# A hybrid decoder step on one core: 16-row instead of 32-row substitution on GpSimd, the keys' norm on ScalarE, and another order of steps

## The chip, the cores and the metric

One core of one Trainium2 chip. The metric is the device time of one execution in microseconds. Engines are called as in the profile: PE (TensorE, matmuls), DVE (VectorE), ACT (ScalarE), POOL (GpSimd), SP (SyncE, which here only issues transfers).

## What is computed

One inference step of a two-layer trunk, for a prompt of 512 tokens and a batch of 8 samples of 4 tokens (544 columns in all, model width 1024). Layer 0 mixes tokens by a gated delta rule (16 value heads, 8 key heads, 128 wide), layer 1 by sliding-window attention; after each comes a SwiGLU block. The delta rule, cut to what the change touches, is computed in chunks:

```
q, k = l2norm(q) * 128**-0.5, l2norm(k)
kb   = k * beta
Bm   = where(strict_lower, (kb @ k.T) * decay, 0)        # one matrix per chunk and head
T    = inverse of (I + Bm)                               # unit lower triangular
u    = T @ (v * beta);   w = T @ (kb * exp(G))
aqk  = (q @ k.T) * decay                                 # lower triangular
# then chunk by chunk, in order:
unew = u - w @ S
o    = (q * exp(G)) @ S + aqk @ unew
S    = S * exp(Gl) + (k * exp(Gl - G)).T @ unew
```

The kernel takes chunks of 128 tokens, so that 4 chunks x 16 heads = 64 matrices T of 128x128 are needed, 16 for each of four groups of 4 heads.

## The kernel before

All large products go through `dense` (L141): weights come by SP from memory in pieces of 128x512 (256 KB, `load_w` L129, three buffers `wr_*`), ACT casts each piece to a high part (`wh_*`, L134), DVE subtracts for the low part (`wl_*`, L136), and PE multiplies at L160 three times (hi x hi, lo x hi, hi x lo) over two halves of 256 and 288 columns. In names, `win` are the projections to q, k, v, `wz` those to the gate z, `wo` the output projection.

Layer 0 is done for four groups g = 0..3 of four heads. The string `PLAN` (L38) names the steps in the order in which the program writes them: `kq` projects queries and keys, `t` (`tphase`, L599) makes the matrices, `p` (`states`) feeds small products with the samples' states between the dense matmuls, `v` projects values, `s` is the sample's part, `m` (`merge`, L776) joins inverted blocks to whole T, `c` (`chain`, L840) goes through the four chunks, `z` projects the gates, `o` (`out`, L1024) normalizes and multiplies them. A tile framework then orders each engine's instructions by its own estimates; waits are semaphores, and an engine never passes an instruction that waits.

What `tphase` does for a group, in turn: PE transposes keys and queries (`pkt`), ACT squares them (`ssk`), 1/norm of the keys comes as `rk` from POOL (`rsqrt_col`, a power, L215), and its logarithm `lk` from ACT. From these DVE makes `cbk`, `ckd`, `R`, `Rh`, `RR`; PE transposes `RR` (`prr`, L663), then makes Gram matrices (`gram`, L685) and decays (`pe`, L689/691); ACT takes exponentials `E` (L697) and DVE writes `BA` (L698, both the matrix to invert and the causal one). SP copies the 32x32 diagonal blocks of `BA` to memory (`D1`, L703) and back with one block on each of 64 partitions, twice (`Lb`, L722). POOL inverts them by forward substitution in `Tn`, even columns on 64 partitions and odd ones on the other 64 (L726 to L735, the loop quoted below). DVE makes a transposed copy (L737, into `Lb`'s memory), SP writes both to memory (`D2`, L742/743) and reads them back in the places that merging needs: three transfers to `Tn` (L748; the tile's second half holds zeros, L745) and eight to `BA` (L752).

```
for j in range(31):
    r_, w = 31 - j, j // 2 + 1
    POOL.tensor_tensor(tv, Lb[:, j, j+1:32] ..., Tn[:, j, 0:w] ..., ALU.mult)
    POOL.tensor_tensor(Tn[:, j+1:32, 0:w], Tn[:, j+1:32, 0:w], tv, ALU.subtract)
```

`merge` works on two halves of a group, eight matrices each: 16 small matmuls `pw` (L791/792) multiply the block below the diagonal with the inverse above it, ACT negates to `W1` (L794), 24 matmuls `py` (L798 to 800) multiply with the other inverse, ACT copies to `BA` and `Tn`; then the same once more from 64 to 128 rows (`pw2` L812, `W2` L814, `py2` L818, `BA` L819). `chain` needs `BA` from its first matmul on (`pu`, L878; then `pS` L883, `po` L849, `pk` L864, `pq` L871).

`out` takes 1/norm of the outputs from POOL as well (`ro`, L1041, the same function at L215), ACT scales `Os` (L1042) and the outputs (L1051, names `KQ`) by it, and POOL issues transfers of results (`out_sp` L892, `out_ss` L1003, `ogsc` L1088).

Of the kernel before, what the change touches and what calls it, by code (L numbers as in the profile page):

```python
# [398 lines left out]
def gdn(ctx, tc, env):  # L399
# [199 lines left out]
    def tphase(q):  # L599
# [127 lines left out]
        for k in range(2):
            POOL.memset(TU[64 * k:64 * k + 64, 16 * k:512:33], 1.0)
        for j in range(31):
            r_, w = 31 - j, j // 2 + 1  # L730
            tt = p2.tile([P, 136], F32, tag="subt", name=f"subt{g}_{j}", bufs=1)
            tv = tt[:, :r_ * w].rearrange("p (a b) -> p a b", b=w)
            POOL.tensor_tensor(tv, Lb[:, j, j + 1:32].unsqueeze(2).to_broadcast([P, r_, w]),  # L733
                              Tn[:, j, 0:w].unsqueeze(1).to_broadcast([P, r_, w]), ALU.mult)
            POOL.tensor_tensor(Tn[:, j + 1:32, 0:w], Tn[:, j + 1:32, 0:w], tv, ALU.subtract)  # L735
# [814 lines left out]
```

## Time and profile before

| what | value |
|---|---|
| timed runs | 1718.17, 1713.74, 1734.78 us; median 1718.17 us |
| the profiled execution | 1713.87 us |
| its span | 1712.1 us |
| mean clock granted to PE in it | 0.971 |
| layer 0's delta part | 0 to about 700 us of the span |

The profile is of one execution. All times of rows are in us from the start of its span, unless ns is written. Nothing behind the first 700 us is touched by the change. The 1.8 us between span and execution time lie around the program.

### The profile page before, as it was taken

To read this page: it belongs to the slowest core of one execution; us is meant where nothing else is said; L and a number is where in the kernel's file an instruction comes from. 1 tells how busy PE (TensorE), PEld (TensorE's weight loads), DVE (VectorE), ACT (ScalarE), POOL (GpSimd) and SP (SyncE) were. 2 spreads that over 40 slices of the span, in tenths; PEclk is the share of its full clock that TensorE was granted. 3 is DMA by queue.
4 is the path that set the end of the run, shared out by engine and by line. 5 is a ranking of instruction groups with operands and counts; after the bars stand their busy time and mean duration, and the time that the engine had idled before them with its cause. 6 is when DMAs were issued, how large, how long until landed. Compare 5 with 4: busy or idle time off the path is not lost.

```text
span 1712.1 us, 34075 instructions
## 1 busy us (share of the span) xinstructions
PE 1614.7 (94%) x13370; PEld 1557.7 (91%) x13370; DVE 946.8 (55%) x2073; ACT 753.8 (44%) x1822; POOL 254.3 (15%) x484
## 2 busy tenths in 40 slices
PE   7997998899698798999999999999989999999997
PEld 6997897799588798999999999999779999999997
DVE  7986486477367456544444433457656444444233
ACT  5865485584565445433333323236544333333221
POOL 2318128117305200100000000000000000000001
PEclk9999899899799999999999999999999999999998
DMA  6224533533455564622222333453112222223322
GB/s 216 81 79 129 134 97 89 154 115 108 110 162 160 155 218 132 196 90 87 92 87 87 89 90 85 119 150 99 57 41 83 88 88 92 87 87 90 90 85 86
DMA packets 155506, 187.73 MB, mean 110 GB/s; under 512 B 59232, under 2 KB 83856, under 8 KB 155344
## 3 DMA queue, kind: packets, MB, share of 16 engines
q1 hardware_dynamic: 146960, 164.34, 32.6%
q0 software_dynamic: 4256, 14.67, 2.5%
q10 hardware_dynamic: 4128, 6.53, 1.3%
q8 instruction: 105, 1.72, 0.4%
q14 instruction: 57, 0.47, 0.1%
HBM read 155.23 MB, written 25.02 MB: 105 GB/s over the span
## 4 chain that ended last, share of the span: by engine, by line
PE 75%; POOL 8%; DMA 5%; DVE 4%; ACT 3%; issue 3%; SPq 1%; ACTq 0%; DVEq 0%; POOLq 0%
PE wu_p L160 15%; PE wg_p L160 15%; PE wd_p L160 14%; PE win_p L160 5%; PE wz_p L160 4%; PE wqkv_p L160 4%; POOL Tn L735 3%; POOL subt L733 3%; PE wao_p L160 3%; PE wo_p L160 2%; DMA xsc<-xr 1%; PE ptp L1279 1%; DMA Lb<-D 1%; PE gram L685 1%; PE po L1285 1%
## 5 line engine op out<-in xcount | busy, mean ns | idle before, releaser
L160 PE MATMUL wg_p<-hl,wh_wg 128*128 128x256 f32 (+1 forms) x704 | 199.8, 288 | 1.5 <-DVE hl L207 1.5
L160 PE MATMUL wu_p<-hl,wh_wu 128*128 128x256 f32 (+1 forms) x704 | 199.7, 288 | 0.0
L160 PE MATMUL wg_p<-hh,wl_wg 128*128 128x256 f32 (+1 forms) x704 | 199.1, 287 | 0.0
L160 PE MATMUL wu_p<-hh,wl_wu 128*128 128x256 f32 (+1 forms) x704 | 199.1, 287 | 0.0
L160 PE MATMUL wg_p<-hh,wh_wg 128*128 128x256 f32 (+1 forms) x704 | 198.5, 288 | 0.3 <-DVE g L330 0.3
L160 PE MATMUL wu_p<-hh,wh_wu 128*128 128x256 f32 (+1 forms) x704 | 198.8, 288 | 0.0
L160 PE MATMUL wd_p<-al,wh_wd 128*128 128x256 f32 (+1 forms) x660 | 190.4, 289 | 0.0
L160 PE MATMUL wd_p<-ah,wl_wd 128*128 128x256 f32 (+1 forms) x660 | 190.1, 288 | 0.0
L160 PE MATMUL wd_p<-ah,wh_wd 128*128 128x256 f32 (+1 forms) x660 | 188.1, 285 | 0.0
L136 DVE TENSOR_TENSOR wl_wd<-wr_wd,wh_wd 128x512 fp32r<-128x512 f32 x90 | 58.3, 648 | 151.8 <-ACT wh_wd L134 150.7
L160 PEld LDWEIGHTS wg_p<-hl,wh_wg 128*128 128x128 f32 x704 | 132.4, 188 | 1.7 <-DVE hl L207 1.7
L134 ACT CAST wh_wg<-wr_wg 128x512 fp32r<-128x512 f32 x88 | 54.7, 621 | 178.6 <-PE wu_p L160 128.0
L160 PEld LDWEIGHTS wg_p<-hh,wh_wg 128*128 128x128 f32 x704 | 132.3, 188 | 0.4 <-DVE g L330 0.4
L160 PEld LDWEIGHTS wg_p<-hh,wl_wg 128*128 128x128 f32 x704 | 132.6, 189 | 0.0
L160 PEld LDWEIGHTS wu_p<-hh,wl_wu 128*128 128x128 f32 x704 | 132.6, 189 | 0.0
L160 PEld LDWEIGHTS wu_p<-hh,wh_wu 128*128 128x128 f32 x704 | 132.4, 188 | 0.0
L160 PEld LDWEIGHTS wu_p<-hl,wh_wu 128*128 128x128 f32 x704 | 132.4, 188 | 0.0
L160 PE MATMUL win_p<-hl0n,wh_win 128*128 128x256 f32 (+1 forms) x448 | 131.7, 296 | 0.6 <-DVE hl0n L279 0.6
L160 PE MATMUL win_p<-hh0n,wl_win 128*128 128x256 f32 (+1 forms) x448 | 131.8, 297 | 0.0
L160 PE MATMUL win_p<-hh0n,wh_win 128*128 128x256 f32 (+1 forms) x448 | 131.2, 295 | 0.5 <-ACT pre L542 0.5
L134 ACT CAST wh_wd<-wr_wd 128x512 fp32r<-128x512 f32 x90 | 52.7, 585 | 174.9 <-PE wd_p L160 154.0
L160 PEld LDWEIGHTS wd_p<-al,wh_wd 128*128 128x128 f32 x660 | 124.1, 188 | 0.0
(453 smaller groups left out, 4489.6 us busy)
## 6 DMA issues: line engine op xcount, KB each, us to landing
wr_wg<-in_w_gu SPq DMA_DIRECT2D x88, 256.0 KB
wr_wu<-in_w_gu SPq DMA_DIRECT2D x88, 256.0 KB
wr_wd<-in_w_dn SPq DMA_DIRECT2D x75, 256.0 KB
wr_win<-in_w_in SPq DMA_DIRECT2D x64, 256.0 KB
Sgp<-in_sdelta SPq DMA_DIRECT2D x16, 512.0 KB
wr_wz<-in_w_in SPq DMA_DIRECT2D x32, 256.0 KB
Sgs<-in_sdelta SPq DMA_DIRECT2D x16, 512.0 KB
out_ss<-Sgs POOLq DMA_DIRECT2D x16, 512.0 KB, 4.2
```

Source lines behind the costliest of these rows:

```text
L134: ACT.copy(hi[:, :n], raw[:, o:o + n])
L136: DVE.tensor_tensor(lo[:, :n], raw[:, o:o + n], hi[:, :n], ALU.subtract)
L160: PE.matmul(ps[f][:m, :hw(f)], lhsT=wt[:, sl], rhs=xt[:, hc(f)], start=(k0 + j == 0 and wi == 0), stop=(k0 + j == total - 1 and wi == 2),)
L685: PE.matmul(gr[:, j * 256:(j + 1) * 256], lhsT=KQ[j][:, n, 0, :], rhs=KQ[j][:, n].rearrange("p a b -> p (a b)"), start=True, stop=True)
L733: POOL.tensor_tensor(tv, Lb[:, j, j + 1:32].unsqueeze(2).to_broadcast([P, r_, w]), Tn[:, j, 0:w].unsqueeze(1).to_broadcast([P, r_, w]), AL ...
L735: POOL.tensor_tensor(Tn[:, j + 1:32, 0:w], Tn[:, j + 1:32, 0:w], tv, ALU.subtract)
L1279: PE.transpose(ptp[:, c * 256 + kb * P:c * 256 + (kb + 1) * P], s[:, c, n, kb * P:(kb + 1) * P], ident)
L1285: PE.matmul(po[rows, n * P:(n + 1) * P], lhsT=vt[:, n - 1 + kb, kv * 64:kv * 64 + 64], rhs=pT[:, c, kb * P:(kb + 1) * P], start=(kb == k0 ...
```

## The change

Four edits, all in layer 0's delta part.

1. Substitution on 16 rows. The tile `LT` holds one 16x16 diagonal block on each of 128 partitions (first half the block, second half its inverse). The loop has 15 steps of two POOL instructions instead of 31. The memory tile `D2` (one for the plain and one for the transposed inverses) is now made once, with zeros between the 16-row blocks, which POOL writes at the program's start; SP reads the inverses back as 32x32 block-diagonal pieces, four transfers to `TU` and one to a new tile `DT` (transposed), and no longer to `BA`.
2. Joining 16 to 32 rows at the start of `merge`: 64 matmuls `pa`, one DVE instruction to `V` (which masks and negates), 112 matmuls `pz`, three DVE additions to `DT` and `TU`, eight POOL copies from `DT` to `BA` for the group. The rest of `merge` reads `DT` where it read the diagonal blocks of `BA`.
3. The keys' 1/norm `rk` is exp(-0.5 * lk) on ACT instead of a power on POOL.
4. Another `PLAN`. Smaller buffers pay for the new tiles (`VBB` 7 instead of 8, one buffer for `R`, `Rh`, `RR`, another tag for two small tiles).

```diff
-PLAN = ("ba kq0 rn gt t0 p0 v0 s0 m0 kq1 v1 c0 t1 p1 z0 kq2 o0 s1 m1 v2 p2 "
-        "c1 t2 z1 o1 kq3 s2 m2 v3 t3 c2 z2 p3 z3 o2 s3 m3 c3 wa wb o3")
+PLAN = ("ba kq0 rn gt t0 p0 kq1 v0 s0 m0 t1 p1 c0 v1 kq2 z0 o0 s1 m1 t2 "
+        "p2 c1 v2 kq3 z1 o1 s2 m2 t3 c2 v3 p3 z2 z3 o2 s3 m3 c3 wa wb o3")
...
+    D2 = [dpool.tile([16, 4, 2, 16, 32], F32, name=f"D2{t}", bufs=1) for t in "nt"]
...
+    zero = big("sub", "zero", 3)
+    POOL.memset(zero[:, :512], 0.0)
+    for t in range(2):
+        nc.gpsimd.dma_start(D2[t].rearrange("u b k s c -> (u b k) (s c)"), zero[:, :512])
...
         rk = p2.tile([P, 9], F32, tag="rk", name=f"rk{g}")
-        rsqrt_col(rk, ssk, 9)
         lk = p2.tile([P, 9], F32, tag="lk", name=f"lk{g}")
         ACT.activation(lk, ssk, AF.Ln)
+        ACT.activation(rk, lk, AF.Exp, scale=-0.5)
...
-        Lb = big("sub", f"Lb{g}", 3)
+        LT = q.LT = p2.tile([P, 2, 16, 16], F32, tag="LT", name=f"LT{g}", bufs=1)
+        Lb, Tn = LT[:, 0], LT[:, 1]
         for k in range(2):
-            nc.sync.dma_start(Lb[64 * k:64 * k + 64], D1.rearrange("b n h s c -> (b n h) (s c)"))
...
+            o = slice(16 * k, 16 * k + 16)
+            nc.sync.dma_start(Lb[64 * k:64 * k + 64], D1.rearrange("u b s c -> (u b) s c")[:, o, o])
         POOL.memset(Tn, 0.0)
+        POOL.memset(Tn.rearrange("p s c -> p (s c)")[:, 0:256:17], 1.0)
+        TU = q.TU = big("sub", f"TU{g}", 3).rearrange("p (u c) -> p u c", c=64)
+        POOL.memset(TU[0:64], 0.0)
+        for j in range(15):
+            r_, w = 15 - j, j + 1
+            tt = p2.tile([P, 64], F32, tag="subt", name=f"subt{g}_{j}", bufs=1)
+            tv = tt[:, :r_ * w].rearrange("p (a b) -> p a b", b=w)
+            POOL.tensor_tensor(tv, Lb[:, j, j + 1:16].unsqueeze(2).to_broadcast([P, r_, w]),
+                              Tn[:, j, 0:w].unsqueeze(1).to_broadcast([P, r_, w]), ALU.mult)
+            POOL.tensor_tensor(Tn[:, j + 1:16, 0:w], Tn[:, j + 1:16, 0:w], tv, ALU.subtract)
+        Tt = Lb
+        DVE.tensor_copy(Tt, Tn.rearrange("p a b -> p b a"))
...
+            for t, src in enumerate((Tn, Tt)):
+                nc.sync.dma_start(D2[t].rearrange("u b k s c -> k (u b) s c")[k][:, :, o], src[64 * k:64 * k + 64])
+        q.DT = p2.tile([P, 16, 32], F32, tag="DT", name=f"DT{g}", bufs=1)
+        nc.sync.dma_start(q.DT, D2[1].rearrange("u b k s c -> (b k s) u c"))
+        for b in range(4):
             o = 32 if b == 1 else 0
...
+            nc.sync.dma_start(TU[32 * b:32 * b + 32, :, o:o + 32], D2[0][:, b].rearrange("u k s c -> (k s) u c"))
...
-        g, TU = q.g, q.TU
+        g, TU, DT = q.g, q.TU, q.DT
+        blocks = [(u_, slice(32 * b, 32 * b + 32)) for u_ in range(16) for b in range(4)]
+
+        pa = bank("v", f"pa{g}")
+        for u_, bs in blocks:
+            o = 32 if bs.start == 32 else 0
+            PE.matmul(pa[bs, u_ * 32:u_ * 32 + 32], lhsT=q.BA[u_ // 8][bs, u_ // 4 % 2, u_ % 4, 0, bs],
+                      rhs=TU[bs, u_, o:o + 32], start=True, stop=True)
+        V = q.LT.rearrange("p a b c -> p (a b c)").rearrange("p (u c) -> p u c", c=32)
+        POOL.memset(V[:, :, 16:32], 0.0)
+        DVE.tensor_scalar(V[:, :, 0:16], pa.rearrange("p (u c) -> p u c", c=32)[:, :, 0:16], kc("partu"), -1.0,
+                          ALU.mult, ALU.mult)
+        pz = bank("v", f"pz{g}")
+        for u_, bs in blocks:
+            PE.matmul(pz[bs, 256 + u_ * 16:272 + u_ * 16], lhsT=V[bs, u_], rhs=DT[bs, u_, 16:32], start=True, stop=True)
+            if bs.start < 96:
+                PE.matmul(pz[bs, u_ * 16:u_ * 16 + 16], lhsT=DT[bs, u_], rhs=V[bs, u_, 0:16], start=True, stop=True)
+        pzv = pz.rearrange("p (t u c) -> p t u c", t=2, c=16)
+        DVE.tensor_tensor(DT[:, :, 16:32], pzv[:, 1], DT[:, :, 16:32], ALU.add)
+        DVE.tensor_tensor(TU[0:96, :, 0:16], pzv[0:96, 0], TU[0:96, :, 0:16], ALU.add)
+        DVE.tensor_tensor(TU[32:64, :, 32:48], pzv[32:64, 0], TU[32:64, :, 32:48], ALU.add)
+        for hf in range(2):
+            for b in (2, 3, 0, 1):
+                bs = slice(32 * b, 32 * b + 32)
+                POOL.tensor_copy(q.BA[hf][bs, :, :, 0, bs].rearrange("p n h c -> p (n h) c"), DT[bs, 8 * hf:8 * hf + 8])
```

Where the instructions now stand. PE before, in the middle of group 1's `tphase`: its first matmul `prr1` stands between dense matmuls of the gate projection z0 (the number behind a name's group is a head's, the last one a buffer's).

```order
L160 MATMUL wz0_2_p1_3154<-hh0n_4_632,wl_wz0_2_0_4_3165 128x288
L663 MATMUL prr1_2699<-kon_70,RR1_2694 68x128
L685 MATMUL gram1_0_2711<-KQ1_1791 128x256 x2
L160 MATMUL wz0_2_p1_3154<-hh0n_5_636,wh_wz0_2_0_4_3163 128x288
L160 MATMUL wz0_2_p1_3154<-hl0n_5_637,wh_wz0_2_0_4_3163 128x288
```

PE of the changed program at the same place (`pa0` is the first matmul of group 0's `merge`, the bulk of it stands here).

```order
L161 MATMUL win4_p0_3321<-hh0n_7_650,wh_win4_0_4_3331 128x256
L161 MATMUL win4_p0_3321<-hl0n_7_651,wh_win4_0_4_3331 128x256
L161 MATMUL win4_p0_3321<-hh0n_7_650,wl_win4_0_4_3333 128x256
L782 MATMUL pa0_1922<-TU0_931,BA0_0_824 32x32 x31
L782 MATMUL pa0_1922<-TU0_931,BA0_1_871 32x32 x32
L670 MATMUL prr1_2336<-kon_70,RR1_2331 68x128
L692 MATMUL gram1_0_2348<-KQ1_1023 128x256 x2
```

Group 0's joining has moved ahead of group 1's `tphase`: 187 dense matmuls (91 of 256 and 96 of 288 columns), 18 transposes and 8 small products stand between the last `pe0` and the first `pa0`; before, 127 `win`, 192 `wz`, 96 state products, `prr1` and a `gram1` stood between the last `pe0` and the first `pw0`.

POOL before, in group 1's substitution: `ro0`, the 1/norm of group 0's outputs, stands between the halves of a step.

```order
L733 TENSOR_TENSOR subt1_21_2882<-Lb1_2812,Tn1_2815 128x110
L735 TENSOR_TENSOR Tn1_2815<-Tn1_2815,subt1_21_2882 128x10x11
L733 TENSOR_TENSOR subt1_22_2885<-Lb1_2812,Tn1_2815 128x108
L215 TENSOR_TENSOR ro0_3704<-sso0_3666,mhalf_73 128x17
L735 TENSOR_TENSOR Tn1_2815<-Tn1_2815,subt1_22_2885 128x9x12
```

POOL of the changed program, from the last step of group 1's substitution to `ro0`.

```order
L741 TENSOR_TENSOR LT1_2449<-LT1_2449,subt1_14_2498 128x15
L556 COPY cso2_3158<-pre4_3383 128x3
L557 COPY cso2_3158<-pre4_3383 128x24
L785 MEMSET LT1_2449 128x16x16
L547 MEMSET pre5_3462 128x3
L548 COPY pre5_3462<-scst2_3159 128x8x3
L556 COPY cso2_3158<-pre5_3462 128x3
L557 COPY cso2_3158<-pre5_3462 128x24
L909 DMA out_sp<-S0_2543 128x4x128
L216 TENSOR_TENSOR ro0_3789<-sso0_3751,mhalf_73 128x17
```

`ro0` now comes after the whole substitution; the memset of `V` (L785) waits until SP's copies of the inverses have been read.

SP before, from group 1's blocks to the copies of its inverses: the weights of z1 are loaded ahead of the copies.

```order
L722 DMA Lb1_2812<-D1_1_2709 64x1024 x2
L129 DMA wr_win27_0_0_4280<-in_w_in 128x512
L129 DMA wr_win27_0_4_4282<-in_w_in 128x512
L129 DMA wr_wz1_0_0_0_4866<-in_w_in 128x512
L129 DMA wr_wz1_0_0_4_4868<-in_w_in 128x512
L129 DMA wr_wz1_1_0_0_4962<-in_w_in 128x512
L129 DMA wr_wz1_1_0_4_4964<-in_w_in 128x512
L900 DMA Sgp1_2_2957<-in_sdelta 128x4x256
L129 DMA wr_wz1_2_0_0_5058<-in_w_in 128x512
L900 DMA Sgp1_3_2959<-in_sdelta 128x4x256
L129 DMA wr_wz1_2_0_4_5060<-in_w_in 128x512
```

SP of the changed program at the same place.

```order
L730 DMA LT1_2449<-D1_1_2346 64x16x16 x2
L748 DMA D2n_192<-LT1_2449 64x16x16 x2
L748 DMA D2t_193<-LT1_2449 64x16x16 x2
L753 DMA TU1_2454<-D2n_192 32x16x32 x3
L750 DMA DT1_2506<-D2t_193 128x16x32
L753 DMA TU1_2454<-D2n_192 32x16x32
L130 DMA wr_wz0_1_0_0_3549<-in_w_in 128x512
L130 DMA wr_wz0_1_0_4_3551<-in_w_in 128x512
```

Nothing stands between `LT1` and the copies of its inverse, so the weights of z0's second head are issued only when the whole substitution and its way back are done. In group 2 the weights of z1's third head, in group 3 those of z3's third head stand behind the copies in the same way.

## Rows read from the trace of the kernel before

**Rows 1.** The page: busy time by engine, and the chain that ended last.
```profile
PE 1614.7 (94%) x13370; PEld 1557.7 (91%) x13370; DVE 946.8 (55%) x2073; ACT 753.8 (44%) x1822; POOL 254.3 (15%) x484
...
PE 75%; POOL 8%; DMA 5%; DVE 4%; ACT 3%; issue 3%; SPq 1%; ACTq 0%; DVEq 0%; POOLq 0%
```

**Rows 2.** Stretches: length, busy of PE, PEld, DVE, ACT, POOL; PE clock, DMA share, GB/s.
```profile
0.00:700.00 700.00, 623.63 (x5407) 582.45 (x5407) 455.16 (x1026) 406.30 (x1152) 233.23 (x445) 0.95 0.46 136
150.00:600.00 450.00, 394.05 (x3549) 365.46 (x3548) 271.93 (x621) 253.11 (x750) 174.61 (x339) 0.92 0.45 127
200.00:250.00 50.00, 48.89 (x381) 42.24 (x380) 37.39 (x92) 36.20 (x106) 7.67 (x21) 0.83 0.42 126
```

**Rows 3.** Waits of PE, 0 to 700 us: total, times, longest.
```profile
PE wz_p L160 <- ACT wh_wz L134: 16.3, 2, 9.1
PE pw L791 <- DMA Tn<-D: 13.9, 4, 6.6
PE prr L663 <- DVE RR L661: 8.7, 1, 8.7
...
PE wo_p L160 <- ACT wh_wo L134: 4.2, 1, 4.2
...
PE pw L792 <- DMA Tn<-D: 1.9, 2, 1.2
```

**Rows 4.** Waits of all engines, 0 to 700 us.
```profile
ACT Os L1042 <- POOL ro L215: 29.3, 3, 12.1
```

**Rows 5.** The chain that ended last, pieces between 126 and 296 us (start, duration).
```profile
127.03 0.41 DVE BA L698
...
135.80 0.67 POOL subt L733
...
163.97 1.79 POOL rk L215
...
177.36 3.69 DMA D<-Tn
...
181.15 4.15 DMA Tn<-D
...
217.75 1.71 PE pu L878 x8
...
227.58 0.89 PE pu L878 x8
...
285.86 3.06 POOL ro L215
```

**Rows 6.** POOL's groups, 0 to 700 us (count, busy us, mean ns, idle before).
```profile
L735 POOL TENSOR_TENSOR Tn<-Tn,subt 128x126 f32<-128x126 f32 (+22 forms) x124 | 68.1, 549 | 8.8
...
L733 POOL TENSOR_TENSOR subt<-Lb,Tn 128x81 f32<-128x81 f32 x4 | 3.3, 826 | 0.3
...
L733 POOL TENSOR_TENSOR subt<-Lb,Tn 128x91 f32<-128x91 f32 x4 | 1.7, 430 | 0.3
...
L735 POOL TENSOR_TENSOR Tn<-Tn,subt 128x16 f32<-128x16 f32 x4 | 0.9, 222 | 0.3
```

**Rows 7.** PE in order of time, 124 to 190 us (start, duration).
```profile
124.89 0.39 PE L691 MATMUL pe<-maskp,identr 128*128 128x512 bf16 x1
...
186.43 0.21 PE L792 MATMUL pw<-Tn,BA 32*32 32x32 f32 x1
...
186.95 0.23 PE L792 MATMUL pw<-Tn,BA 32*32 32x32 f32 x2
...
187.33 0.28 PE L160 MATMUL win_p<-hh0n,wl_win 128*128 128x256 f32 x1
...
189.33 0.28 PE L160 MATMUL win_p<-hl0n,wh_win 128*128 128x256 f32 x1
```

**Rows 8.** Waits of SP's queue, 0 to 700 us.
```profile
SPq L129 <- DVE wl_wz L136: 67.0, 19, 12.8
```

**Rows 9.** SP's transfers in order of time, from 295 us (start, duration of issuing).
```profile
296.50 1.63 SPq L742 DMA_DIRECT2D D<-Tn  x2
```

More of the change, by code (lines that the diff above doesn't have):

```diff
@@ L33 @@
 SGB = 2
+VBB = 7
 KQB = 3
@@ L676, in tphase @@
         q.BA = []
-        D1 = dpool.tile([4, NCH, 4, 32, 32], F32, tag="D1", name=f"D1_{g}")
+        D1 = dpool.tile([16, 4, 32, 32], F32, tag="D1", name=f"D1_{g}")
         for hf in range(2):
@@ L726, in tphase @@
         POOL.memset(Tn, 0.0)
-        for k in range(2):
[L728 to L735, printed above, removed]
@@ L736, in tphase @@
-        Tt = Lb.rearrange("p s c -> p (s c)")[:, :512].rearrange("p (c s) -> p c s", s=32)
-        DVE.tensor_copy(Tt, Tn.rearrange("p a b -> p b a"))
-        D2 = dpool.tile([2, 4, NCH, 4, 32, 32], F32, tag="D2", name=f"D2_{g}")
-        for k in range(2):
-            ks = slice(64 * k, 64 * k + 64)
-            nc.sync.dma_start(D2[0].rearrange("b n h s c -> (b n h) s c")[:, :, 16 * k:16 * k + 16], Tn[ks])
-            nc.sync.dma_start(D2[1].rearrange("b n h (s k) c -> k (b n h) s c", k=2)[k], Tt[ks])
@@ L781, in merge @@
             us = [(n2, h, 8 * hf + 4 * n2 + h) for n2 in range(2) for h in range(4)]
-            def plain(t):
-                return t.rearrange("p (b k c) -> p b c k", k=2, c=16)
-            W1 = p2.tile([P, 8, 32], F32, tag="E", name=f"W1{g}_{hf}", bufs=2)
+            W1 = q.LT[:, hf].rearrange("p (u a) c -> p u (a c)", a=2)
             pw = bank("v", f"pw{g}_{hf}")
@@ L790, in merge @@
                 c = slice(i * 32, i * 32 + 32)
-                PE.matmul(pw[32:64, c], lhsT=ba[0:32, n2, h, 0, 32:64], rhs=plain(TU[0:32, u_, 0:32]), start=True, stop=True)
-                PE.matmul(pw[96:128, c], lhsT=ba[64:96, n2, h, 0, 96:128], rhs=plain(TU[64:96, u_, 0:32]), start=True, stop=True)
+                PE.matmul(pw[32:64, c], lhsT=ba[0:32, n2, h, 0, 32:64], rhs=TU[0:32, u_, 0:32], start=True, stop=True)
+                PE.matmul(pw[96:128, c], lhsT=ba[64:96, n2, h, 0, 96:128], rhs=TU[64:96, u_, 0:32], start=True, stop=True)
             for r in (32, 96):
@@ L805, in merge @@
             ACT.copy(ba[0:32, :, :, 0, 32:64], v8c(py[0:32, 0:256]))
-            ACT.copy(TU[32:64, 8 * hf:8 * hf + 8, 0:32].rearrange("p u (k c) -> p u c k", k=2),
-                     py[32:64, 0:256].rearrange("p (u c k) -> p u c k", u=8, k=2))
+            ACT.copy(TU[32:64, 8 * hf:8 * hf + 8, 0:32], py[32:64, 0:256].rearrange("p (u c) -> p u c", u=8))
             ACT.copy(ba[64:96, :, :, 0, 96:128], v8c(py[64:96, 0:256]))
@@ L811, in merge @@
                 c = slice(i * 64, i * 64 + 64)
-                PE.matmul(pw2[64:128, c], lhsT=ba[0:64, n2, h, 0, 64:128], rhs=plain(TU[0:64, u_, :]), start=True, stop=True)
+                PE.matmul(pw2[64:128, c], lhsT=ba[0:64, n2, h, 0, 64:128], rhs=TU[0:64, u_, :], start=True, stop=True)
             W2 = p2.tile([P, 8, 64], F32, tag="un", name=f"W2{g}_{hf}", bufs=1)
@@ L822, in proj_v @@
         g = q.g
-        q.Vb = [p2.tile([P, 4, P], F32, tag="Vb", name=f"Vb{g}_{n}", bufs=8) for n in range(NCH)]
+        q.Vb = [p2.tile([P, 4, P], F32, tag="Vb", name=f"Vb{g}_{n}", bufs=VBB) for n in range(NCH)]
         q.VS = p2.tile([P, 4, NB, NT], F32, tag="VS", name=f"VS{g}")
@@ L957, in sample @@
         g = q.g
-        ksT = p2.tile([P, 256], F32, tag="E", name=f"ksT{g}", bufs=2)
+        ksT = p2.tile([P, 256], F32, tag="ksT", name=f"ksT{g}", bufs=1)
         for f in range(2):
```

33 lines of the change are left out of this document (10 added, 23 removed).

## The prediction

> **What bounds the kernel now.** I read the page first. PE is busy for 94% of the span and holds 75% of the chain that ended last, and POOL, busy for only 15%, holds 8% of that chain [rows 1]. A lightly used engine with such a share stands somewhere in PE's way, so the question is where. The stretches come next: from 0 to 700 us, the only part that the change touches, PE is busy for 623.63 us [rows 2], so 76.4 us are idle, while the rest of the span is nearly full. A second loss is the clock. From 150 to 600 us PE had 0.92 of it [rows 2]; of its two levels, 1.2 and 2.4 GHz, it was then at the lower for 16% of the time, 72 us, which cost half of that, 36 us. In the stretch from 200 to 250 us, where group 0's small matmuls of joining run, PE was busy for 48.89 of 50 us and yet had 0.83, a loss of 8.5 us without any wait [rows 2]. That leaves about 27 us that may have to do with waits.
>
> The list of PE's waits names them [rows 3]. For 16.3 us the gate projections `wz` wait for ACT's casts, for 4.2 us `wo` does; 8.7 us go to `prr`, once; 13.9 and 1.9 us to `pw`, which waits for inverses coming back from memory. What the first name hides is told by ACT's own waits: `Os`, which stands before those casts on ACT, waits 29.3 us for POOL's `ro` [rows 4]. And the chain of waits shows why `ro` is late: it takes 3.06 us at 285.86, in the middle of group 1's substitution, as `rk` (1.79 us at 163.97) stands in the middle of group 0's [rows 5]. POOL runs these long loops alone: 124 subtractions of 549 ns in the mean [rows 6], and as many products. So 45.0 us of PE's idle time (16.3 + 4.2 + 8.7 + 13.9 + 1.9) come from the length of the substitution, and from what has to pass POOL behind it.
>
> **The change part by part.** *The keys' norm on ACT.* `rk` leaves POOL, and the 8.7 us of `prr` go: ACT makes it in one instruction on 9 columns directly behind `lk`. What is late next there is discussed with `pa`, since `prr1` now stands behind it on PE. Counted: -8.7.
>
> *The shorter substitution.* 30 instructions of 15 to 64 elements replace 62 of 16 to 136. Their price lies between the undisturbed 222 ns of the 128x16 form and the mean of 549 ns [rows 6]; with some 70 ns between two instructions (the chain shows 0.67 us at 135.80 for a first one of 31 elements that should take much less, so the disturbance matters [rows 5]) I take 0.46 us a step, 13.8 us a group, with 9 and 18 as ends. `ro0` is then no longer inside a substitution, and for groups 1 to 3 inverses come back before `pw` asks. The waits behind `ro` (20.5) and on the inverses (15.8) go. Counted: -36.3. If the cover fails, they return, which is rival C.
>
> *The clock.* Of the 27 us, I count the part that goes with the idle time that really goes: 45.0 less the 20.5 that is added below, over 76.4, times 27: -9, with 0 and -27 as ends.
>
> *More matmuls.* Four groups get 64 `pa` and 112 `pz`. The nearest row is `pw`: 16 matmuls in two strips of the array lie between 186.43 and 186.95 [rows 7], 33 ns each, so 66 ns in one strip. With four strips side by side that is 16.5 ns, 2.9 us a group, +12 in all. The ends are 33 ns (+23) and, since most `pz` are 16 columns wide and not 32, half of mine (+6). The Trainium skill, page "TensorEngine Tiling (Array Packing)", section Instruction Overhead, gives some 60 cycles to each matmul however narrow; at 2.4 GHz that is an estimate of 25 ns each, 17.6 us in all and a sum 6 us higher. The row's 33 ns for a matmul in two strips agrees with a fixed price per matmul, and whether four strips share it no row shows.
>
> *A new wait at group 0's joining.* This is where the order matters. Between the last `pe0` and the first `pa0` PE now has 91 dense matmuls of 256 and 96 of 288 columns. Seventeen of 256 took 2.00 us from 187.33 to 189.33 [rows 7], 0.118 each, so 0.133 for the wide ones: 10.7 + 12.8 = 23.5 us, and with the 26 transposes and small products some 27.7. The chain against it starts at the same point: from `pe` at 124.89 [rows 7] to the last `BA`, ending at 127.44, 2.5 us; to the first step at 135.80, 8.4 us for two trips through memory [rows 5]; 13.8 us of steps; the transposed copy and four issues, 0.8 each by SP's pair of 1.63 us [rows 9], some 2.7; then landings of 3.69 and 4.15 us [rows 5]. Together 35.3, and with 0.2 between them 35.5: `pa0` waits for 8 us, 4 with the fast steps and 12 with the slow ones. Queued behind it on PE are `prr1` and all of group 1's `tphase`, so the wait is paid in full: +8. In groups 1 to 3 the same count of matmuls gives covers of about 55, 44 and 42 us, enough for 35.5.
>
> *Hops inside joining.* `V`, three additions, then `pw`: PE has little else between them in group 0 (one `prr`, one `gram`, one `pe`). By the 0.41 us that `BA`, 128x256, took on DVE [rows 5], four of these are 1.6 us a group, 6.6 in all. Eight POOL copies of 256 elements at 0.22 to 0.83 us [rows 6] run beside `pw`, `W1` and `py`, but stand behind transfers of results that wait for DVE; I add 1.4. Counted: +8, between 0 (all under dense matmuls) and 20 (four copies in the open in each group).
>
> *SP's order.* The weights of z0's second head stand behind the copies of group 1's inverses. They can be issued some 35.5 us behind the last `pe1`. Before PE needs them, it has 72 dense matmuls of `win` and 48 of `wz` (15.2 us) and three rounds of the chain; a round from one `pu` to the next took 9.8 us, from 217.75 to 227.58 [rows 5], with dense work in it, so the cover lies between 15 + 3 x 5 and 15 + 3 x 7, and I take 34. With landing and cast the wait is 3.5 us, 0 to 9. SP's loads already wait 67 us for free buffers [rows 8], which costs PE nothing as long as two pieces are ahead; here none are. Groups 2 and 3 have one such load each, for +1 together. Counted: +4.5.
>
> The zeros that POOL writes at the start, the smaller buffers and the moved `kq` steps I cost at nothing: POOL has idle time there, and dense matmuls cover it.
>
> **Sum.** -8.7 - 36.3 - 9 + 12 + 8 + 8 + 4.5 = -21.5. Against the profiled execution's 1713.9 us that is 1692. The median of the runs shown is 4 us above that execution, so a median after could lie as much above my number.
>
> **The rivals.** *B, the covers hold and the clock is full.* Fast steps (222 ns) make `pa0` wait 4 us, SP is never late (0), the matmuls cost 12 and the hops 6, and the clock gives all 27: -45 - 27 + 12 + 6 + 4 = -50, 1664 us. For it speaks that nearly every wait in the list has its cause on POOL [rows 3, 4]; against it the stretch with 0.83 and no idle time [rows 2], which more small matmuls could only lengthen.
>
> *C, the waits only move.* The clock gives nothing, since idle time is replaced by small matmuls; `pa0` waits 10, the hops cost 14, SP's order 6: -45 + 12 + 10 + 14 + 6 = -3, 1711 us. For it: 176 tiny matmuls a group with three DVE hops between. Against it: the substitution does become shorter by half in every group.
>
> *D, slower: POOL's steps are dragged out.* Two forms of nearly one size took 826 (81 elements) and 430 ns (91 elements) [rows 6]; the time of a step is set by what runs beside it. At 0.9 us a step the substitution takes 27 us, 13.2 longer. `pa0` then waits 21 instead of 8 (+13), z0's weights come 14 later than counted (+14, since the cover there is used up), and in groups 2 and 3 covers of 44 and 42 fail by 5 and 7 (+12): 1692 + 39 = 1731 us. It decides from about 0.76 us a step, where the delays have eaten the 21.5. The Trainium skill, page "SBUF — State Buffer", section Who interferes with whom, states that a DVE instruction with two inputs in SBUF contends with a GpSimd instruction that reads SBUF. The subtractions that make `wl_*` are such, and the pair of forms above agrees with it; in group 0's substitution, now under dense `win` work alone, they would be as dense as before. By the mean of 549 ns over all forms [rows 6] the effect is in my 0.46 only in part.
>
> **How the numbers follow.** The forecast has 0.52, with 1678 to 1704 as its own range (steps, matmuls and hops each at half their distance to an end); B 0.21, C 0.17, D 0.10. The range that leaves out 2 in 10 goes from 1662 to 1722. A measurement of this kernel can tell about 2% from no change (34 us here). Faster by more means below 1680: B, and the lower end of the forecast, 0.29. Slower by more means above 1748: only a D with more than 0.9 us a step, 0.04. Within: 0.67.
>
> **What would show it.** In the profile after, `prr` and the waits of `wz`/`wo` behind `ro` should be gone from PE's list, and a wait of `pa` on a transfer (one of some 8 us, in group 0 alone) should be new. `pa` and `pz` should take 2 to 4 us a group. POOL's steps should average 0.4 to 0.5 us, and a `wz0_1` cast should be waited for by 3 or 4 us. The clock from 150 to 600 us should be 0.93 to 0.95. The prediction is wrong if PE's idle time before 700 us is under 45 us (B) or still over 60 (C, D), or if waits of `pz`, `pw` or `py2` on DVE and POOL add up to more than 15 us.

## The result, and the profile after

The changed kernel took 1700.0 us (median of 4 runs, 1693.84 to 1707.14), the kernel before 1716.0 us beside it: a ratio of 0.9884, with an interval from 0.984 to 0.9928. A second set gave 0.9879 (0.9853 to 0.9904). The ratios are of a set's runs and lie a little lower than those of its medians (0.9907 here), so the gain is 16 us by the medians and 20 by the ratio. The forecast, 1692 of 1713.9 us, was a ratio of 0.987. Both profiled executions are less far apart, 1703.09 and 1713.87 us, mostly by the clock: before's had a mean granted clock of 0.971, better than the 0.966 to 0.967 in the middle of its timed runs, the changed kernel's had 0.972, against 0.973.

First the page of the changed kernel: busy time, and the chain that ended last.

```profile
PE 1634.9 (96%) x14778; PEld 1574.8 (93%) x14778; DVE 942.4 (55%) x2089; ACT 753.6 (44%) x1826; POOL 178.9 (11%) x387
...
PE 82%; DMA 5%; DVE 4%; issue 3%; ACT 2%; POOL 2%; SPq 1%; POOLq 0%; ACTq 0%; DVEq 0%
```

Against [rows 1], POOL fell from 8% to 2% of the chain, and PE took its place. The stretches (columns as in [rows 2]) up to the first matmul of the SwiGLU block, before and after, and the place of group 0's joining and group 1's `tphase`, before and after:

```profile
0.00:694.40 694.40, 618.03 (x5362) 576.93 (x5363) 452.27 (x1021) 403.08 (x1147) 233.23 (x445) 0.95 0.46 134
160.00:200.00 40.00, 31.32 (x290) 29.56 (x291) 14.78 (x39) 12.22 (x27) 14.02 (x36) 0.87 0.40 93
```

```profile
0.00:684.70 684.70, 635.61 (x6770) 591.27 (x6771) 449.06 (x1038) 403.08 (x1152) 157.91 (x348) 0.95 0.46 135
160.00:200.00 40.00, 34.01 (x557) 25.91 (x557) 17.49 (x61) 11.37 (x28) 6.97 (x13) 0.59 0.52 150
```

PE idled for 49.1 us instead of 76.4, 27.3 less, and was busy for 17.6 us more; the difference, 9.7 us, is nearly all that the profiled pair gained (10.8). In the profiled execution of the second set PE idled for 43.8 us. Between 160 and 200 us the clock fell from 0.87 to 0.59. The waits of PE, 0 to 700 us, of the changed kernel, to be held against [rows 3]:

```profile
...
PE pSs L1014 <- DVE Sgs L1018: 4.2, 4, 2.2
PE pz L790 <- issue: 3.8, 2, 2.8
PE pa L782 <- DMA TU<-D2n: 3.3, 1, 3.3
PE win_p L161 <- DVE wl_win L137: 3.0, 2, 2.5
PE pSs L1014 <- ACT Ue L1007: 2.9, 3, 1.8
...
PE py L816 <- ACT LT L812: 2.5, 1, 2.5
...
PE wz_p L161 <- ACT wh_wz L135: 1.0, 1, 1.0
```

All 45.0 us of [rows 3] are gone but for 1.0 at `wz`. What is new is many and small: `pa` waits once for 3.3 us, joining's hops show as `pz` (3.8 and 0.6), `py` and 0.2 at `pw`, and the samples' products `pSs` wait 7.1 us where they waited 0.6 before. POOL's groups show the shorter loop: 120 instructions of some 340 ns, where 248 had about 530 [rows 6].

```profile
L739 POOL TENSOR_TENSOR subt<-LT 128x15 f32<-128x15 f32 (+7 forms) x60 | 21.0, 349 | 45.4 <-DMA LT<-D 41.3
L741 POOL TENSOR_TENSOR LT<-LT,subt 128x15 f32<-128x15 f32 (+7 forms) x60 | 19.6, 327 | 4.4
```

### The profile page after: what moved, and what is told of

Its sections match the earlier page's. It is cut to its first block, busy times and chain, and to the rows that moved or that the text cites. A ratio compares the mean times of both kernels' runs of the same rounds, so it can differ in the third digit from the quotient of the medians.

```text
span 1701.3 us, 36800 instructions
## 1 busy us (share of the span) xinstructions
PE 1634.9 (96%) x14778; PEld 1574.8 (93%) x14778; DVE 942.4 (55%) x2089; ACT 753.6 (44%) x1826; POOL 178.9 (11%) x387
## 4 chain that ended last, share of the span: by engine, by line
PE 82%; DMA 5%; DVE 4%; issue 3%; ACT 2%; POOL 2%; SPq 1%; POOLq 0%; ACTq 0%; DVEq 0%
PE wg_p L161 16%; PE wu_p L161 16%; PE wd_p L161 14%; PE win_p L161 6%; PE wo_p L161 6%; PE wz_p L161 4%; PE wqkv_p L161 4%; PE wao_p L161 3%; PE ptp L1296 1%; PE po L1302 1%; PE gram L692 1%; PE wdl_p L374 1%; DMA wk<-ksd 1%; PE pu L895 1%; PE po L866 1%
## 5 line engine op out<-in xcount | busy, mean ns | idle before, releaser
L161 PE MATMUL win_p<-hl0n,wh_win 128*128 128x256 f32 (+1 forms) x448 | 136.9, 307 | 1.6 <-DVE hl0n L280 1.4
L161 PE MATMUL win_p<-hh0n,wh_win 128*128 128x256 f32 (+1 forms) x448 | 135.2, 304 | 0.0
```

The lines of the kernel that those rows point to most:

```text
L161: PE.matmul(ps[f][:m, :hw(f)], lhsT=wt[:, sl], rhs=xt[:, hc(f)], start=(k0 + j == 0 and wi == 0), stop=(k0 + j == total - 1 and wi == 2),)
```

## The experiments

Theory A: the length of the substitution on POOL made PE's waits, so the 16-row blocks are what gains, less what joining costs. Theory P: the new order of steps gains, the substitution doesn't. In the table, the clock's loss is the span times one minus the run's mean granted clock (at 1.2 GHz half of the time counts as lost), and the rest is the span times the clock; both are medians over the timed runs. The rows of before are from the same sets. It is a split of the time, not a cause: a wait that ends at the lower clock lies in both. Where a profile is shown, it is of one execution, and the clock differs from one to the next.

| run | median us | ratio (interval) | span x clock | clock's loss |
|---|---|---|---|---|
| before (four sets) | 1716.2 to 1718.6 | 1 | 1657 to 1659 | 57 to 58 |
| changed (two sets) | 1700.0, 1698.5 | 0.9884, 0.9879 | 1651, 1648 | 46, 48 |
| rk on ACT alone | 1715.9 | 0.9986 (0.997 to 1.0003) | 1658 | 57 |
| new order + rk, 32 rows | 1725.6 | 1.0051 (1.0032 to 1.007) | 1653 | 70 |
| 16 rows + rk, old order | 1704.6 | 0.9917 (0.9891 to 0.9942) | 1656 | 48 |
| changed, no joining | 1669.4 | 0.9717 (0.9691 to 0.9742) | 1629 | 39 |
| changed, joining's matmuls twice | 1743.0 | 1.0135 (1.0104 to 1.0166) | 1667 | 73 |
| changed, `pz` in another order | 1696.6 | 0.9872 (0.9846 to 0.9899) | 1649 | 49 |
| that, z0 early (two sets) | 1691.9, 1696.3 | 0.9847 (0.9821 to 0.9873), 0.9883 (0.9851 to 0.9914) | 1655, 1653 | 35, 40 |
| z0 early, no joining | 1680.3 | 0.9775 (0.9742 to 0.9807) | 1634 | 45 |
| before, rk and ro on ACT | 1714.6 | 0.9981 (0.9961 to 1.0001) | 1656 | 58 |
| changed, longer substitution | 1710.7 | 0.9959 (0.9936 to 0.9982) | 1652 | 59 |

**One part alone: rk on ACT.**

```diff
-        rsqrt_col(rk, ssk, 9)
         ACT.activation(lk, ssk, AF.Ln)
+        ACT.activation(rk, lk, AF.Exp, scale=-0.5)
```

> The kernel before with one edit of the change alone: rk as exp(-0.5 lk) on ACT. If the length of the substitution on POOL is the cause of PE's waits (theory A), the 8.7 us of prr in group 0 go, and POOL has 1.8 us less in each substitution; the waits of wz and wo behind ro and of pw on the inverses stay at about 36 us: 1706 to 1712 us. If the order of the steps is the cause (theory P), the prr wait turns into another one close behind it: 1714 to 1718 us.

It took 0.14% off, 2.4 us (0.3 by the medians), not clear of nothing. The wait of `prr` did go. Its waits of PE, 0 to 700 us, and two rows of DVE:

```profile
PE pw L791 <- DMA Tn<-D: 16.9, 4, 8.2
PE pkt L609 <- ACT Kt L615: 8.8, 1, 8.8
...
PE wz_p L160 <- ACT wh_wz L134: 7.2, 1, 7.2
PE wo_p L160 <- ACT wh_wo L134: 5.6, 1, 5.6
PE win_p L160 <- DVE z L1021: 5.2, 1, 5.2
```

```profile
172.57 0.59 DVE L737 COPY Lb<-Tn 128x512 f32<-128x512 f32 x1 [10.09 <-POOL Tn L735]
...
173.74 0.41 DVE L1021 SCALAR_TENSOR_TENSOR z<-zt,wz_p 128x256 f32<-128x256 f32 x1
```

The time is in theory P's range, and A's 4 to 10 us were a miss. In group 0, where `prr` had waited, PE now waits 5.2 us at a `win` matmul for DVE's `z`, and `z` stands on DVE behind the transposed copy of the inverses (L737), which had waited 10.09 us for the last step of the substitution. So the wait moved, but to another thing behind the same loop. The `pkt` wait is not its successor: it lies at 295.9 us, behind ACT's scaling by `ro`, in the place of one of the two waits of `wz`. What A wanted to see stay (`wz`, `wo`, `pw`, now with `pkt`) adds up to 38.5 us, near its 36.

**Edits 3 and 4 without the substitution.** The diff is the one above with the new PLAN.

> The kernel before with the new order of steps and rk on ACT, but still the substitution on 32 rows. Theory A: ro of groups 0 and 1 still stands inside substitutions, and pw of group 0, which now has about 44 us of PE work against a chain of some 60 us, waits about 16 us, so the new order gives nothing without the shorter substitution: 1710 to 1730 us, and over 30 us of PE waits behind POOL. Theory P: the order makes the gain, and the substitution gives nothing: 1698 to 1706 us.

1725.6 us: A's range, and well off P's. The waits of PE, 0 to 700 us, and the stretch from 160 to 200 us:

```profile
PE pSs L997 <- ACT Ue L990: 14.1, 4, 11.7
PE pw L791 <- DMA Tn<-D: 12.3, 4, 5.5
```

```profile
160.00:200.00 40.00, 19.73 (x182) 15.31 (x182) 14.69 (x48) 9.89 (x23) 15.75 (x39) 0.55 0.46 119
```

With the long loop, PE stands for half of this stretch, and has 0.55 of the clock in it. The longest wait, 11.7 us of `pSs`, hangs on the same copy on DVE: it ended at 177.95 us, the last step of the substitution at 175.1. With the 4.1 us of `pw` behind it that is A's 16 us for group 0. Against the run with `rk` alone, the new order makes the kernel slower by some 0.6%, by the split all of it in the clock's loss, 70 instead of 57.

**The substitution without the new order.**

```diff
-PLAN = ("ba kq0 rn gt t0 p0 kq1 v0 s0 m0 t1 p1 c0 v1 kq2 z0 o0 s1 m1 t2 "
+PLAN = ("ba kq0 rn gt t0 p0 v0 s0 m0 kq1 v1 c0 t1 p1 z0 kq2 o0 s1 m1 v2 p2 "
...
```

> The changed kernel with the old order of steps: the substitution on 16 rows, the joining and rk on ACT stay. Theory A: the 45 us of waits go here as well, since ro now stands behind each substitution and the covers are 46.7, 44, 45 and 37 us against a chain of 35.5 us; 19 us of joining matmuls and some 10 us of hops are added: 1688 to 1702 us, no wait of pa in group 0. Theory P: without the new order the added matmuls eat the gain: 1710 to 1720 us.

A ratio of 0.9917, some 14 us less than before (11.6 by the medians): 1704.6 us, 2.6 over A's range and 5 under P's. Its stretch from 160 to 200 us:

```profile
160.00:200.00 40.00, 38.02 (x664) 32.62 (x662) 22.16 (x71) 15.80 (x36) 7.31 (x15) 0.91 0.57 174
```

In the old order, 120 dense matmuls stand between the small ones here, where the changed kernel has 13, and the clock keeps 0.91. A was wrong in one point: `pa` still waits, 9.3 us in six places, group 0's among them. By the two pairs, the 16 rows give 0.7% in the old order (0.9917 against 0.9986) and 1.7% in the new one (0.988 against 1.0051). The new order gives some 6 us with 16 rows, which the intervals just don't part, and takes 10 with 32. So the shorter substitution gains in both orders, which is theory A, and the order alone doesn't, against P.

**Joining left out.** The 176 matmuls of a group, the instructions to `V` and the three additions are gone.

```diff
-        pa = bank("v", f"pa{g}")
...
-        DVE.tensor_tensor(TU[32:64, :, 32:48], pzv[32:64, 0], TU[32:64, :, 32:48], ALU.add)
```

> The changed kernel without the joining of 16 to 32 rows: the matmuls pa and pz, the instruction to V and the three additions are left out; substitution, transfers and the POOL copies stay. It measures what joining costs. Theory A: 19 us of issue time of pa and pz on PE, 7 to 10 us of waits of pa, pz and pw, and some 4 us of lower clock in group 0 go: 1668 to 1680 us. Rival (joining lies in time in which PE would have waited anyway, for transfers or the chain): 1688 to 1700 us.

1669.4 us: joining costs 1.6 to 1.7%, 28 to 31 us, and A's range was met. By the split, 18 to 22 us lie at full clock and 7 to 9 in the clock. The clock of this place is low all the same:

```profile
160.00:200.00 40.00, 35.91 (x304) 27.74 (x305) 18.06 (x61) 17.05 (x40) 7.43 (x15) 0.53 0.48 141
```

So the low stretch is there without joining's matmuls as well, though this execution was the slowest of six (1679.2 us at a mean clock of 0.967, the others 1667.8 to 1671.4 at 0.976 to 0.978), and in the others it may be shorter. What both have is the new order, which runs the rest of group 0's `merge` and group 1's `tphase` here with hardly any dense work between.

**Joining's matmuls doubled, their order, and z0 early.** Three runs beside the changed kernel.

```diff
+        for u_, bs in blocks:
+            o = 32 if bs.start == 32 else 0
...
+        for u_, bs in blocks:
+            PE.matmul(pz[bs, 256 + u_ * 16:272 + u_ * 16], lhsT=V[bs, u_], rhs=DT[bs, u_, 16:32], start=True, stop=True)
...
```

> The changed kernel with each matmul of pa and pz issued twice: 704 more matmuls in all, no further hop. Theory M (joining costs its matmuls, some 25 to 32 ns each as they stand, four strips or not): 18 to 23 us more than the changed kernel, a ratio to the kernel before of about 1.000 (0.998 to 1.004). Theory H (the cost left out in the run without joining was mostly hops, waits and the change between tile sizes, and the matmuls themselves share the strips at 10 to 16 ns): 7 to 11 us more, a ratio of 0.992 to 0.996.

Both theories were too low: 44.5 us more than the changed kernel beside it. By the split 19 us lie at full clock, 27 ns for each of 704 matmuls, which is M's size; another 25 us are the clock. Up to the first SwiGLU matmul it had 0.90 of it, the changed kernel 0.94 in the same set:

```profile
0.00:732.00 732.00, 670.54 (x8178) 623.38 (x8179) 452.81 (x1038) 404.75 (x1152) 159.10 (x348) 0.90 0.43 127
```

```profile
0.00:683.50 683.50, 639.69 (x6771) 594.40 (x6772) 449.28 (x1037) 403.56 (x1152) 159.61 (x348) 0.94 0.46 135
```

The order of `pz`:

```diff
-        for u_, bs in blocks:
+        for u_ in range(16):
+            for b in range(4):
...
+            for b in range(3):
```

> The changed kernel with the 112 pz matmuls of a group written in another order: for each of the 16 units first the four with V as weights, one in each strip, then the three with DT, so that two neighbours never share a strip. If neighbours in one strip wait for each other, pz falls from some 16 to 20 ns per record towards the 10 ns of group 3, 3 to 6 us less: ratio 0.984 to 0.987. If the strips do not matter: within 1 us of the changed kernel.

1.8 us less than the changed kernel beside it, between both answers and within the intervals; that neighbours don't share a strip is worth little.

```diff
-PLAN = ("ba kq0 rn gt t0 p0 kq1 v0 s0 m0 t1 p1 c0 v1 kq2 z0 o0 s1 m1 t2 "
+PLAN = ("ba kq0 rn gt t0 p0 kq1 v0 z0 s0 m0 t1 p1 c0 v1 kq2 o0 s1 m1 t2 "
```

> As the run with the other order of pz, and with PLAN changed so that z0 comes ahead of s0 and m0: 16 to 23 of every 26 instructions on PE around group 0's joining and group 1's gram and pe are then dense matmuls (none before). If the long stretch at the lower clock (171 to 201 us in the changed kernel, 161 to 198 without joining) comes from PE running small work alone there, it shrinks to under 10 us, which gives 8 to 12 us back; against it, pa of group 1 now has a short cover and waits some 10 us on its transfers: ratio 0.983 to 0.990. If the clock does not follow that work, the stretch stays over 25 us and the ratio is 0.990 to 0.995.

> The changed kernel itself once more, on the same chip as the three beside it, as their measure: ratio 0.985 to 0.992. Theory A and theory P differ in how it stands to the old order with the same substitution (0.9917): A expects it within 4 us of that, P at least 8 us faster.

The first set gave 1691.9 us, 6.6 under the changed kernel beside it and 4.8 under the run with the other order of `pz`, which differs in `PLAN` alone, in the first branch's range. The clock's loss fell from 49 to 35 us. The low stretch got shorter, but not under 10 us: in this execution it lasted 20.5 us (170.6 to 191.1), which lies between the two branches. The 10 us that `pa` of group 1 was to wait did not come; all waits of `pa` add up to 3.1 us, and they lie in group 0. At full clock z0 early is 7 us worse in this set. The changed kernel itself, 0.9879, stands 6 us under the old order's 0.9917, between what A (4) and P (8) expected of it. The same kernel in another set:

> The run with z0 ahead of the joining once more, as the measure for the one beside it and as the version that may beat both kernels: 1688 to 1695 us, ratio 0.982 to 0.987, a clock of 0.70 to 0.95 between 160 and 200 us, where the changed kernel had 0.59.

1696.3 us and 0.9883, a miss upwards, with the clock as expected. Its stretch from 160 to 200 us:

```profile
160.00:200.00 40.00, 38.41 (x600) 32.88 (x601) 25.75 (x77) 17.79 (x39) 8.84 (x22) 0.74 0.55 172
```

Over both sets it can't be told from the changed kernel, so no version here is shown to beat it. Beside it ran the same without joining:

> The run with z0 ahead of the joining, without the joining of 16 to 32 rows (pa, pz, V and the three additions left out). It asks whether the 28 us that joining cost in the changed kernel belong to the place where it stood (at the lower clock, with no dense work near) or to the instructions. If to the instructions (some 21 us of PE's time at full clock and a few of waits): 24 to 29 us under the run beside it that joins, 1663 to 1668 us. If to the place: under 18 us, above 1673 us.

1680.3 us, 16 less, in the range of the place. By the split, joining costs 20 us at full clock here too (1653 against 1634), while the clock's loss goes the other way, 45 without and 40 with it. From 160 to 200 us, and from 294 to 339 us, this run had:

```profile
160.00:200.00 40.00, 38.21 (x409) 33.50 (x409) 30.30 (x79) 23.39 (x54) 11.33 (x30) 0.93 0.56 181
294.20:339.40 45.20, 34.76 (x245) 26.39 (x244) 26.73 (x69) 23.86 (x68) 4.64 (x10) 0.70 0.33 107
298.70:326.00 27.30, 23.18 (x168) 17.11 (x169) 14.34 (x43) 10.78 (x24) 4.26 (x7) 0.50 0.40 137
```

The same 45 us in the run beside it, with joining:

```profile
294.20:339.40 45.20, 44.16 (x392) 38.20 (x390) 30.60 (x73) 29.37 (x76) 7.68 (x19) 1.00 0.50 159
```

So leaving joining out also changed the order elsewhere: from 294 to 339 us PE now had no dense matmul, waited 8.4 us in one place, and had the lower clock for 27.3 us; with joining it had the full clock all through. The 16 us hold this loss too, so the run doesn't part place from instructions. What both pairs show alike is some 20 us at full clock, wherever joining stands.

**Queue or length.** In the kernel before, `rk` and `ro` of groups 0 to 2 on ACT.

```diff
-            rsqrt_col(ro, sso, 17)
+            ACT.activation(ro, sso, AF.Ln)
+            ACT.activation(ro, ro, AF.Exp, scale=-0.5)
```

> The kernel before (32 rows, old order) with rk on ACT and, besides, ro of groups 0 to 2 on ACT (ln, then exp), so that nothing that PE needs stands inside a substitution; 8 more table loads on ACT are the price. It parts two ways in which the long substitution can cost time. Theory Q (its place in POOL's queue: ro waits behind it): the 13 us that wz and wo still waited with rk alone go, some 5 us come back through ACT, 1700 to 1710 us. Theory L (its own length: the inverses come late): pw's waits of some 17 us stay or grow by what went elsewhere, 1711 to 1718 us.

1714.6 us, theory L's range. Its waits of PE, 0 to 700 us:

```profile
PE wz_p L160 <- DVE wl_wz L136: 8.8, 2, 8.6
...
PE pw L791 <- DMA Tn<-D: 7.3, 3, 4.6
PE pks L935 <- DVE r L931: 7.0, 2, 5.8
PE pks L935 <- DVE r L932: 6.5, 1, 6.5
```

Neither `rk` nor `ro` stands inside a substitution any more, and the waits behind ACT's casts are gone, yet others of the same sum came, behind DVE. What they hang on stands in DVE's own waits, and in its rows where the wait of 8.6 us ends:

```profile
DVE Lb L737 <- POOL Tn L735: 30.6, 4, 10.1
```

```profile
292.71 0.59 DVE L737 COPY Lb<-Tn 128x512 f32<-128x512 f32 x1 [8.19 <-POOL Tn L735]
293.22 1.30 DVE L136 TENSOR_TENSOR wl_wz<-wr_wz,wh_wz 128x512 fp32r<-128x512 f32 x2
```

DVE reaches the transposed copy of the inverses early and stands there until POOL's last step, 30.6 us in four places where the kernel before had 4.2. Behind it on DVE wait `wl_wz` (8.6 us of PE), `z` (5.1) and `r` (5.8 and 6.5): 26.0 us. So L's cause is shown, the length of the loop, but not its way: `pw`'s waits didn't stay at 17, they fell to 7.3, and the length is paid through DVE's queue.

**A longer substitution.** Each product is issued three times.

```diff
+            for _ in range(3):
-            POOL.tensor_tensor(tv, Lb[:, j, j + 1:16].unsqueeze(2).to_broadcast([P, r_, w]),
+                POOL.tensor_tensor(tv, Lb[:, j, j + 1:16].unsqueeze(2).to_broadcast([P, r_, w]),
...
```

> The changed kernel with the product of each substitution step on POOL issued three times: 30 more instructions of the same kind in each group, 0.42 us each with the gap, so some 12.6 us more per substitution, the rest as it is. It measures the slope of rival D of the prediction. Theory A (a longer substitution is paid in group 0's pa and in SP's held weight loads): 12 us at pa and some 10 us in the loads and later groups, 1712 to 1728 us, ratio 0.998 to 1.006. Rival (covers are ample, 12.6 us more is hidden but for group 0's 3.3 us wait): under 1704 us, ratio below 0.992.

It took 1710.7 us, some 12 more than the changed kernel and just under A's range; the rival's was passed by more. POOL's group of products:

```profile
L740 POOL TENSOR_TENSOR subt<-LT 128x15 f32<-128x15 f32 (+7 forms) x180 | 61.0, 339 | 44.5 <-DMA LT<-D 31.6
```

That is 40 us of busy time more in four groups, with 120 gaps of 70 ns 48 us, and a quarter of it reached the end, by the split nearly all of it as the clock's loss (59 against 46 to 48). A's 12 us at `pa` did not come: the framework had moved the bulk of group 0's `pa` behind `prr1` and group 1's first Gram matrices and decays in this kernel, and `pa` waits nowhere. Why the clock was lower stays open.

## Why the prediction was right, and where it was not

The time and the ratio were right, and so was the main mechanism: the waits behind the substitution went, and joining gave back more than half (28 to 31 of some 48 us). That the sum came out so close is in part luck. By the split, 6 to 10 us of the gain lie at full clock, where the terms other than the clock's forecast 12.5, and 10 to 12 in the clock, for which 9 had been set by a rule that doesn't hold. Term by term:

- **The removed waits, -45.0.** Gone in the changed kernel, all but 1.0. But the prediction took them as independent, and they are not: without the shorter substitution, -8.7 for `prr` was worth 2.4 us, and with `ro` off POOL too it was 3. With one wait removed, the engines came earlier to the next thing behind the same loop, DVE to its copy of the inverses above all. The sum held since the length, their common cause, was cut. PE's idle time fell by 27.3 us against a forecast of 24.5 (45.0 less 20.5). It was 49.1 us; the 43.8 of the second set lie just under the 45 that were named as a sign of B, yet B's full clock did not come with them.
- **The new wait at `pa`, +8.** It was 3.3. The cover was as counted, 27.9 us from the last `pe0` at 129.48 to the wait at 157.4. The chain was 31.2, not 35.5: 11.2 to the first step (counted 10.9), 13.5 for the steps (13.8), and 6.5 instead of 10.5 for the way back. The landings were taken from the old, larger transfers (3.69 and 4.15 us, [rows 5]); the new ones landed in 2.70 and some 2 us. (The 2.7 us for the copy and four issues were added up too low, since four issues at 0.8 are 3.3 alone; it made no difference.) These are `pe0`'s and `pa`'s rows on PE, and the chain's pieces between them:

```profile
129.48 0.39 PE L698 MATMUL pe<-maskp,identr 128*128 128x512 bf16 x1
...
160.63 0.28 PE L782 MATMUL pa<-TU,BA 32*32 32x32 f32 x2 [3.27 <-DMA TU<-D2n]
```

```profile
137.38 3.13 DMA LT<-D
...
140.65 0.74 POOL subt L739
...
154.28 0.47 SPq L748
...
156.23 2.70 DMA D2t<-LT
```

- **Matmuls +12 and hops +8.** Together 20, and joining measured 18 to 22 us at full clock. The parts were not right: doubling gave 19 us at full clock for the matmuls alone, and the hops show as 7.1 us of waits at `pz`, `py` and `pw`, of which some would stand elsewhere without joining (the run without it waits 4.7 us at `pw` for ACT). PE was busy with `pa` and `pz` for 20.6 us in the changed kernel (columns PE, PEld, DVE), 4.2 to 6.4 a group where 2 to 4 were forecast:

```profile
0.00:700.00 700.00, 7.30 (x512) 5.86 (x512) 1.90 (x4) 0.95 0.47 137
0.00:700.00 700.00, 13.31 (x896) 11.62 (x896) 4.67 (x12) 0.95 0.47 137
```

So the matmuls are the term that was mis-sized, but not by the estimate that four strips run at twice the pace of two. Packed closely at full clock, 33 `pa` (66 records, two each) started within 0.58 us, 17.5 ns each, and group 3's 112 `pz` took 2.1 us, 19 ns each, where two strips gave 33 [rows 7]. By these rows all four groups would take 13 us. They took more because most of them did not run so: in groups 0 to 2 above all they stand in short runs between other work, in part at the lower clock. The Trainium skill, page "TensorEngine Tiling (Array Packing)", section Instruction Overhead, has some 60 cycles a matmul, which the prediction worked out, as an estimate, to 25 ns. Where strips run side by side the packed rows lie under that, and the 27 ns of the doubling, which include the spaces between short runs, near it.

```profile
406.42 0.77 PE L782 MATMUL pa<-TU,BA 32*32 32x32 f32 x66
```

```profile
549.38 0.26 PE L790 MATMUL pz<-DT,LT 32*32 32x16 f32 x7
...
551.47 0.18 PE L792 MATMUL pz<-LT,DT 32*32 32x16 f32 x1
```

- **SP's order, +4.5.** PE's waits for weights are 3.0 at `win` and 1.0 at `wz` in the whole part. The weights of z0's second head were issued at 236.28 us, right behind the copies, and the first was cast at 239.44; PE did not wait at `wz` between 225 and 300 us, so of the 3.5 us counted here nothing came. The 1.0 at `wz` lies at 537 us.
- **The clock, -9.** The loss fell by 10 to 12 us over the timed runs. The size was right, the rule was not: it scaled the clock with PE's idle time and left the new order's effect on it at nothing. Two executions of the second set idle alike, 43.8 us in the changed kernel and 44.8 with z0 early, at mean clocks of 0.968 and 0.977. The trace's record of the clock shows two parts. In the kernel before, seven of eight low stretches up to 700 us, 58 us in all, began during or just behind a wait of [rows 3]; in the changed kernel the short ones add up to 34 and, in the second set, 31 us. Against that, the one stretch in which PE was busy for most of the time grew from 17 to 31 and 48 us. Here it is, before and in the changed kernel's first set:

```profile
204.40:221.50 17.10, 16.84 (x116) 12.98 (x115) 9.56 (x27) 10.34 (x28) 1.99 (x3) 0.50 0.58 187
```

```profile
170.50:201.30 30.80, 28.39 (x388) 20.61 (x391) 14.07 (x45) 9.52 (x25) 6.97 (x13) 0.50 0.46 143
```

Half of each is lost, so by these executions some 12 to 14 us were won behind the waits, more than forecast, and 7 to 15 went to a term that the prediction didn't have. That the 10 to 12 us of the timed runs lie by the 9 is luck.
- **Rival D.** An instruction of the loop took 0.41 us with its gap, against 0.46 assumed. Some were dragged out all the same: 16 of 120 took over 0.5 us, up to 1.01, and each of these stood beside a DVE instruction such as `wl_win<-wr_win,wh_win` or `y<-pre,y`; the 63 with no DVE instruction beside them took 0.21 to 0.32. Two neighbours of 15 elements on POOL, and what ran on DVE beside the second:

```profile
215.34 0.24 POOL L739 TENSOR_TENSOR subt<-LT 128x15 f32<-128x15 f32 x1 [13.06 <-DMA LT<-D]
215.65 0.84 POOL L741 TENSOR_TENSOR LT<-LT,subt 128x15 f32<-128x15 f32 x1
```

```profile
215.72 0.68 DVE L571 SCALAR_TENSOR_TENSOR y<-pre,y 128x512 f32<-128x512 f32 x1
```

This agrees with the Trainium skill's rule (page "SBUF — State Buffer", section Who interferes with whom), but it was too rare to decide anything. The pair of forms in the prediction was put down to the wrong instructions: in the kernel before, the long ones of 81 elements stood beside `r` and `y`, none beside a `wl_*`. D's slope was wrong also: it charged 39 us for 13.2 us a group. The run with the longer loop, in which a substitution took 24 to 28 us, is D's case, and it cost some 12. The covers of groups 1 to 3 were as counted or longer (62.9, 47.1 and 43.0 us from the last `pe` to the first `pa`), but the chain against them was shorter, 29 to 33 us: in the changed kernel the last inverse was issued 34, 16 and 16 us ahead of its `pa`, and with the longer loop still 27, 13 and 8, so no `pa` waited.

## What to carry to other kernels

Waits in a list that have one cause go together or not at all: moving `rk` off POOL, and then `ro` too, gave 2 to 3 us, though 9 and 20 us of waits stood behind them; the cut of the cause gave 14 to 20. To find the cause, follow each new wait back: here ACT, PE and DVE all stood behind one loop on POOL. When work is handed from a slow engine to PE as many tiny matmuls, the pace of a packed run is the least that they cost; look whether they will run packed, and at which clock. An order that gains with a short chain can lose with a long one, so order and length have to be tried as a pair.
